# Written order on ACT, DVE and SP beside PE, and another order of the seven products, in a decoder block on one Trainium2 core

## The chip, the core and the metric

The kernel runs on one core of a Trainium2 chip. The core has five engines with a queue each: PE (TensorE, matmuls), ACT (ScalarE), DVE (VectorE), POOL (GpSimd) and SP (SyncE), and 16 DMA engines that move data between HBM and the on-chip memory. The metric is the device time of one execution, in microseconds. Timed twice, the kernel before took 1585.59 us in the median (1584.92 and 1586.26).

## What is computed

One decoder layer on 256 positions of 2048 channels, in float32:

```python
h = rmsnorm(x, norm_g)
proj = h @ w_in                          # 2048 x 18432, cut into 14 pieces
ya = stick_breaking(a_q, a_k, a_v)                       * silu(a_g)   # 8 heads of 128
yb = silu(layernorm(causal_conv31(b_a * sigmoid(b_b))))  * silu(b_g)
yc = gelu(c_u) * (tril(sgu_w) @ layernorm(gelu(c_v)) + sgu_b) * silu(c_g)
yd = dilated_mixture(d_q, d_k, d_v)                      * silu(d_g)   # 3 groups x 8 heads
gates = sigmoid(h @ w_gate + b_gate)     # 2048 x 8192, one gate per branch and channel
merged = sum(gates[n] * (y[n] @ w_branch[n]) for n in "abcd")
return rmsnorm(x + merged @ w_out, final_g)
```

In the stick-breaking attention `w[t, s]` is beta(t, s) times the product of 1 - beta(t, j) over s < j < t; it needs softplus and a running sum over keys. The dilated mixture is a softmax over three strided sets of keys.

## The kernel before

**Weights.** All weights are cut into 256 tiles of 128 x 2048 float32 (1 MB). A tile is loaded into one of six `st` buffers by a DMA that SP issues (`load_weights`, L85), and split into two float32r parts (`split`, L96): ACT copies it to `hi` (L97), DVE writes `lo = st - hi` (L98), with three buffers for each. A product then takes hi*hi + lo*hi + hi*lo.

**Kinds of work on PE.** `mm_t` (L212) multiplies one tile with all of `h` to give 128 channels of a projection, transposed: 16 pairs of a 512-column matmul (L219) and a 256-column one (L222). `proj_t` (L234) does two such tiles, adds the two halves of the result on DVE (L243) after a copy on ACT (L242), applies the activation functions, and calls `step`. `mm_n` (L251) is used where positions are the rows: four blocks of weights times two blocks of positions times three parts, 24 matmuls (L259 to L261), for the first projection `d_v`, the branches and the output.

**The seven products.** The gates (`gate_group`) and the projections `a_v` and `c_v` (`v_group`) go through `group` (L324). It forms a 2 x 2 block product with seven block products instead of eight, in Winograd's way: the sums s1, s2, s3, n4 of blocks of `h` are made once (`make_sx`, L293), the sums of weight tiles by DVE (`add_to`, L340; L342) in place, in the two tiles `ts` that a group holds to its end. Each product takes two halves of 12 matmuls (`half`, L331; L337), so a group has 14 halves; there are ten groups. The accumulators are X, Z and Y, in PSUM; `keep` (L344) copies one to an `so` buffer (five of them) by ACT and `done` (L350) adds or subtracts the rest on DVE (L353). `group` is a generator; `step(n)` runs n halves from the front of `queue`, so halves are mixed among other work: six per `proj_t` in head 7 and in the `b_g` gates, three per `proj_t` in the a heads, one per tile in the branches, one or two per `proj_t` in the `c_u` and `c_g` projections. What is left in the queue is run without other work between.

**Order of the whole.** The `d_v` projection and the norm (`make_h`, L183); the projections for the convolution, whose 248 taps DVE works off in between; the eight dilated heads (`d_head`, L556), the convolution's norm (`conv_norm`, L619) and `make_sx` among them; the `b_g` gates; branch d; the a heads in pairs (`a_pair`, L676); branches b and a; the norm of `c_v` (L731 to L754) and `c_mix`; branch c, whose sums are transposed by `turn` (L782); the output projection, `finish` and `store`. A branch (`branch`, L464) reads its y back from DRAM in one piece (`yf`), splits it into `yh` and `yl` (in the two `ph` buffers), and adds gate times product to a running sum in DRAM; the gates come back as `gl`, the sum as `ml`, by DMAs that POOL issues.

**What sets the order.** PE runs in the order in which the program is written. For ACT, DVE, SP and POOL a planner in the compiler chooses the order, by its own model of the times and by priorities that the program gives: `SPLIT_AHEAD` 100 for splits and evictions, `ADD_AHEAD` 140 for the sums of tiles, `CHAIN_AHEAD` 600 for the small stages that `later` and `tick` put off by some projections, `CONV_BEHIND` 100 below the rest for the taps. The result is a fixed list for each engine; an engine runs its list in order.

Of the kernel before, what the change touches and what calls it, by code (L numbers as in the profile page):

```python
# [9 lines left out]
F32 = mybir.dt.float32  # L10
# [16 lines left out]
SPLIT_AHEAD = 100  # L27
CHAIN_AHEAD = 600
ADD_AHEAD = 140
CONV_BEHIND = 100  # L30
# [27 lines left out]
def hybrid_block(ctx: ExitStack, tc, w, x, xT, vec, bg, cst, dmask, sgu_wT, sgu_lg, sgu_lb, sgu_b, final_g, out):  # L58
# [21 lines left out]
    ctx.enter_context(tc.manual_schedule(engines={mybir.EngineType.PE}))  # L80
# [3 lines left out]

    def load_weights(expect, pieces=1, between=None, again=False):  # L85
        assert again == (expect in used), expect
        used.add(expect)
        st = st_p.tile([P, 2048], F32, tag="st", name="st")
        n = 2048 // pieces
        for c in range(pieces):  # L90
            nc.sync.dma_start(st[:, c * n:(c + 1) * n], w[index[expect]][:, c * n:(c + 1) * n])
            if between is not None:
                between(c)
        return st
# [5 lines left out]
    def new_hi():  # L100
        return hi_p.tile([P, 2048], F32R, tag="hi", name="hi")[:]

    def new_lo():
        return lo_p.tile([P, 2048], F32R, tag="lo", name="lo")[:]

    def split_tile(st):
        hi, lo = new_hi(), new_lo()
        with tc.high_priority(SPLIT_AHEAD):
            split(hi, lo, st[:])
        return hi, lo  # L110

    def next_weights(expect):
        return split_tile(load_weights(expect))

    pending = []

    def later(n, fn):

        pending.append([n, fn])

    def tick():
        due = []
        for e in list(pending):
            e[0] -= 1
            if e[0] <= 0:
                pending.remove(e)
                due.append(e[1])
        for fn in due:
            with tc.high_priority(CHAIN_AHEAD):
                fn()  # L130

# [51 lines left out]
    def make_h():  # L183

        nc.sync.dma_start(cst_sb[:], cst[:, 0:C_K])
        red, rd2 = (so_p.tile([P, 2, S], F32, tag="so", name=n) for n in ("red", "rd2"))
# [6 lines left out]
        yield  # L193
# [4 lines left out]
        for q in range(4):  # L198
            for k in range(4 * q, 4 * q + 4):
                xk = xt[k // 8][:, k % 8, :]  # L200
                V.scalar_tensor_tensor(xk, xk, norm_g(k), rstd[:], op0=ALU.mult, op1=ALU.mult)
            ks = slice(4 * q, 4 * q + 4)
            split(xhl[:, ks, 0:S], xhl[:, ks, S:2 * S], xt[q // 2][:, 4 * (q % 2):4 * (q % 2) + 4, :])
        yield
# [4 lines left out]
        yield  # L209
# [24 lines left out]
    def proj_t(e0, e1, funcs=(None, None), n=0):  # L234

        dst = qk_p.tile([P, 2, S], F32, tag="qk", name="dst")
        for j, e in enumerate((e0, e1)):
            ps = ps_t.tile([P, 512], F32, tag="t", name="ps")
            mm_t(ps, next_weights(e), xhl)
            with tc.high_priority(SPLIT_AHEAD):  # L240
                bt = ev_p.tile([P, S], F32, tag="bt", name="bt")
                A.activation(bt[:], ps[:, S:2 * S], AF.Copy)  # L242
                V.tensor_add(dst[:, j, :], ps[:, 0:S], bt[:])  # L243
                if funcs[j] is not None:
                    A.activation(dst[:, j, :], dst[:, j, :], funcs[j])
            step((n + 1) // 2 if j == 0 else n // 2)
        tick()
        return dst
# [22 lines left out]
    def first_weights(q, expect):  # L271

        if q == 0:
            st = load_weights(expect, 4, lambda c: load_x(2 * c, 2) if c < 2 else None)
        elif q == 1:
            st = load_weights(expect, 2, lambda c: load_x(4 + 4 * c, 4))
        else:
            st = load_weights(expect, 1, lambda c: load_x(12, 4) if q == 2 else None)
        n = 512 if q == 0 else 1024
        hi, lo = new_hi(), new_lo()  # L280
        for o in range(0, 2048, n):
            for k in range(n // 512):
                split_x(4 * q + o // 512 + k)
            split(hi[:, o:o + n], lo[:, o:o + n], st[:, o:o + n])
        return hi, lo
# [7 lines left out]
    def make_sx():  # L293

        def quarter(k0, t0, name):
            q = st_p.tile([P, KB, P], F32, tag="st", name=name)
            V.tensor_add(q[:], xhl[:, k0:k0 + KB, t0:t0 + P].bitcast(F32), xhl[:, k0:k0 + KB, S + t0:S + t0 + P].bitcast(F32))
            return q
# [6 lines left out]
        a21 = quarter(0, P, "a21")  # L305
        a11 = quarter(0, 0, "a11")
        a22 = quarter(KB, P, "a22")
        V.tensor_sub(a22[:], a21[:], a22[:])
        put("s1", a22[:])
        V.tensor_sub(a22[:], a22[:], a11[:])  # L310
        put("s2", a22[:])
        V.tensor_sub(a11[:], a11[:], a21[:])
        put("s3", a11[:])
        a12 = quarter(KB, 0, "a12")
        V.tensor_add(a12[:], a12[:], a22[:])
        put("n4", a12[:])
# [7 lines left out]
    def group(expect, sink, bias=None):  # L324


        def tile_of(c, h, j):
            e = expect(c, 2 * h + j)
            return load_weights(e, again=e in used)

        def half(ps, st, name, j, first, last):  # L331
            lh = x_part(name)
            hi, lo = split_tile(st)
            for kk in range(4):
                k, o = 4 * j + kk, kk * 512
                for i, (part, w_) in enumerate(((0, hi), (0, lo), (1, hi))):
                    T.matmul(ps[:], lh(k, part), w_[:, o:o + 512], start=first and j == kk == i == 0,  # L337
                             stop=last and j == 1 and kk == 3 and i == 2, skip_group_check=name not in ("a11", "s1", "a12"))

        def add_to(st, other):  # L340
            with tc.high_priority(ADD_AHEAD):
                V.tensor_add(st[:], st[:], other[:])  # L342

        def keep(ps, name):  # L344
            t = so_p.tile([P, 512], F32, tag="so", name=name)
            with tc.high_priority(SPLIT_AHEAD):
                A.activation(t[:], ps[:], AF.Copy)
            return t

        def done(tb, c, op, a, b, t):  # L350
            with tc.high_priority(SPLIT_AHEAD):
                if op is not None:
                    op(t[:], a[:], b[:])  # L353
                sink(tb, c, t, op is not None)

        X = ps_x.tile([P, 512], F32, tag="x", name="X")
        if bias is not None:
            T.matmul(X[:], sel[:, bias:bias + 1].to_broadcast([P, P]), bgr[:], start=True, stop=False)
        ts = []
        for j in range(2):  # L360
            ts.append(tile_of(0, 0, j))
            half(X, ts[j], "a11", j, bias is None, True)
            yield
        p1 = keep(X, "p1")
        Z = ps_n.tile([P, 512], F32, tag="n", name="Z")
        if bias is not None:
            T.matmul(Z[:], sel[:, bias + 8:bias + 9].to_broadcast([P, P]), bgr[:], start=True, stop=False)
        for j in range(2):
            add_to(ts[j], tile_of(1, 0, j))
            half(Z, ts[j], "s1", j, bias is None, True)  # L370
            yield
        p5 = keep(Z, "p5")
        for j in range(2):
            add_to(ts[j], tile_of(1, 1, j))
            half(X, ts[j], "s2", j, False, True)
            yield
        u2 = keep(X, "u2")
        for j in range(2):
            t3, b22 = tile_of(1, 0, j), tile_of(1, 1, j)
            half(Z, b22, "n4", j, False, True)  # L380
            add_to(t3, b22)
            yield
            half(X, t3, "s3", j, False, True)
            if j == 0:
                yield
        done(0, 1, V.tensor_sub, Z, u2, u2)
        done(1, 1, V.tensor_sub, p5, X, p5)
        yield
        Y = ps_n.tile([P, 512], F32, tag="n", name="Y")
        for j in range(2):  # L390
            b21 = tile_of(0, 1, j)
            half(Y, b21, "a12", j, True, True)
            add_to(ts[j], b21)
            yield
            half(X, ts[j], "a22", j, False, True)
            if j == 0:
                yield
        done(0, 0, V.tensor_add, Y, p1, p1)
        done(1, 0, None, X, X, X)
        yield  # L400

    queue = []

    def step(n=1):

# [518 lines left out]
```

## Time and profile before

| | |
|---|---|
| median of two runs | 1585.59 us |
| the profiled execution, and its span | 1585.26 us, 1583.4 us |
| PE busy | 1465.1 us (93%) |
| DVE busy | 1241.8 us (78%) |
| ACT busy | 864.5 us (55%) |
| POOL busy | 87.5 us (6%) |
| granted TensorE clock, mean | 0.969 |
| moved by DMA | 370.89 MB, 234 GB/s over the span |

The span runs from the first to the last instruction of the program. Busy times come from the profiled execution. Matmuls are pipelined and overlap, so a busy PE need not be PE at its peak. In a row of instructions the name left of `<-` is the tile written, those right of it are read; `x320` is a count, then come busy microseconds, the mean nanoseconds of one, and the engine's idle time just before them with what ended it.

### The profile page before, as it was taken

To read this page: it belongs to the slowest core of one execution; us is meant where nothing else is said; L and a number is where in the kernel's file an instruction comes from. 1 tells how busy PE (TensorE), PEld (TensorE's weight loads), DVE (VectorE), ACT (ScalarE), POOL (GpSimd) and SP (SyncE) were. 2 spreads that over 40 slices of the span, in tenths; PEclk is the share of its full clock that TensorE was granted. 3 is DMA by queue.
4 is the path that set the end of the run, shared out by engine and by line. 5 is a ranking of instruction groups with operands and counts; after the bars stand their busy time and mean duration, and the time that the engine had idled before them with its cause. 6 is when DMAs were issued, how large, how long until landed. Compare 5 with 4: busy or idle time off the path is not lost.

```text
span 1583.4 us, 18121 instructions
## 1 busy us (share of the span) xinstructions
PE 1465.1 (93%) x7204; PEld 1225.5 (77%) x7204; DVE 1241.8 (78%) x1232; ACT 864.5 (55%) x777; POOL 87.5 (6%) x159
## 2 busy tenths in 40 slices
PE   7999999999999999869999999989989899959897
PEld 6788887888887777658788788867768688847786
DVE  7799999555799998867788788898889777866454
ACT  6544444353457567644466766766554477744251
POOL 0100000000000000010100000000211200011000
PEclk9999999999999999989999999989999999979999
DMA  9655543555166768677876757677898877578441
GB/s 358 217 211 186 186 176 136 180 180 181 59 237 257 283 249 289 212 276 275 283 282 224 241 213 279 239 260 256 301 337 297 328 274 248 196 282 299 167 161 54
DMA packets 62836, 370.89 MB, mean 234 GB/s; under 512 B 8128, under 2 KB 8256, under 8 KB 24096
## 3 DMA queue, kind: packets, MB, share of 16 engines
q1 hardware_dynamic: 44640, 313.68, 54.9%
q0 software_dynamic: 12784, 46.61, 8.8%
q10 hardware_dynamic: 5328, 9.45, 1.7%
q8 instruction: 56, 0.92, 0.2%
q14 instruction: 28, 0.23, 0.0%
HBM read 343.50 MB, written 26.21 MB: 233 GB/s over the span
## 4 chain that ended last, share of the span: by engine, by line
PE 62%; DVE 14%; DMA 10%; issue 7%; ACT 6%; POOL 0%; DVEq 0%; ACTq 0%; POOLq 0%; SPq 0%
PE ps L219 24%; PE ps L222 12%; DVE lo L98 8%; PE X L337 7%; DMA st<-in_w_dram 6%; ACT hi L97 3%; DVE st L342 3%; PE Z L337 3%; PE Y L337 2%; PE pso L261 2%; PE pso L260 2%; PE pso L259 2%; PE psy L259 1%; PE psy L260 1%; PE psy L261 1%
## 5 line engine op out<-in xcount | busy, mean ns | idle before, releaser
L98 DVE TENSOR_TENSOR lo<-st,hi 128x2048 fp32r<-128x2048 f32 (+2 forms) x318 | 711.6, 2247 | 165.7 <-ACT hi L97 164.9
L97 ACT ACTIVATE hi<-st 128x2048 fp32r<-128x2048 f32 (+2 forms) x318 | 595.0, 1879 | 231.4 <-PE psy L261 83.1
L219 PE MATMUL ps<-xhl,hi 128*128 128x512 f32 x1920 | 691.8, 403 | 6.3 <-ACT vd L523 3.8
L222 PE MATMUL ps<-xhl,lo 128*128 128x256 f32 x1920 | 523.4, 283 | 11.3 <-DVE lo L98 11.3
L219 PEld LDWEIGHTS ps<-xhl,hi 128*128 128x128 f32 x1920 | 361.6, 190 | 86.8 <-ACT vd L523 4.2
L222 PEld LDWEIGHTS ps<-xhl,lo 128*128 128x128 f32 x1920 | 366.2, 191 | 24.3 <-DVE lo L98 14.8
L242 ACT ACTIVATE bt<-ps 128x256 f32<-128x256 f32 x120 | 46.0, 384 | 331.0 <-PE ps L219 329.4
L342 DVE TENSOR_TENSOR st<-st 128x2048 f32<-128x2048 f32 x80 | 182.9, 2287 | 33.9 <-DMA st<-in_w_dram 33.5
L337 PE MATMUL X<-hi,xhl 128*128 128x512 f32 x320 | 109.2, 406 | 12.8 <-ACT hi L97 10.9
L337 PE MATMUL X<-hi,s 128*128 128x512 f32 x320 | 106.0, 393 | 0.9 <-ACT hi L97 0.9
L259 PE MATMUL psy<-hi,yh 128*128 128x512 f32 x256 | 100.6, 393 | 5.2 <-DVE ml L792 4.7
L260 PE MATMUL psy<-lo,yh 128*128 128x512 f32 x256 | 100.7, 393 | 1.6 <-DVE lo L98 1.6
L261 PE MATMUL psy<-hi,yl 128*128 128x512 f32 x256 | 100.2, 392 | 0.0
L243 DVE TENSOR_TENSOR dst<-ps,bt 128x256 f32<-128x256 f32 x120 | 50.5, 420 | 61.9 <-ACT bt L242 61.5
L543 DVE SCALAR_TENSOR_TENSOR cv<-glu,vec_sb,cv 128x246 f32<-128x246 f32 (+27 forms) x240 | 98.8, 462 | 0.2
L337 PEld LDWEIGHTS X<-hi,xhl 128*128 128x128 f32 x320 | 63.2, 197 | 27.2 <-ACT hi L97 11.6
L337 PE MATMUL X<-lo,xhl 128*128 128x512 f32 x160 | 65.1, 407 | 7.0 <-DVE lo L98 7.0
L337 PEld LDWEIGHTS X<-hi,s 128*128 128x128 f32 x320 | 60.7, 190 | 13.5 <-ACT hi L97 1.3
L337 PE MATMUL X<-lo,s 128*128 128x512 f32 x160 | 63.5, 397 | 5.6 <-DVE lo L98 5.6
L337 PE MATMUL Y<-hi,xhl 128*128 128x512 f32 x160 | 59.0, 432 | 3.4 <-ACT hi L97 3.4
L337 PE MATMUL Z<-hi,s 128*128 128x512 f32 x160 | 53.7, 400 | 8.7 <-ACT hi L97 8.7
L259 PEld LDWEIGHTS psy<-hi,yh 128*128 128x128 f32 x256 | 48.4, 189 | 16.3 <-DVE ml L792 4.9
(248 smaller groups left out, 1531.6 us busy)
## 6 DMA issues: line engine op xcount, KB each, us to landing
st<-in_w_dram SPq DMA_DIRECT2D x294, 1024.0 KB, 5.4
gl<-g_dr POOLq DMA_DIRECT2D x32, 256.0 KB, 6.8
m_dr<-gl POOLq DMA_DIRECT2D x24, 256.0 KB, 6.1
ml<-m_dr POOLq DMA_DIRECT2D x24, 256.0 KB, 6.3
g_dr<-p ACTq DMA_DIRECT2D x16, 256.0 KB, 4.5
g_dr<-u ACTq DMA_DIRECT2D x8, 256.0 KB, 5.2
g_dr<-g ACTq DMA_DIRECT2D x8, 256.0 KB, 3.9
xr<-in_x_dram POOLq DMA_DIRECT2D x8, 256.0 KB, 4.4
```

What stands on the lines that cost most here:

```text
L97: A.activation(hi, src, AF.Copy)
L98: V.tensor_sub(lo, src, hi.bitcast(F32))
L219: T.matmul(ps[:], hi[:, o:o + P], rhs[:, k, :], start=start, stop=stop)
L222: T.matmul(ps[:, 0:S], lo[:, o:o + P], rhs[:, k, 0:S], start=False, stop=False)
L242: A.activation(bt[:], ps[:, S:2 * S], AF.Copy)
L243: V.tensor_add(dst[:, j, :], ps[:, 0:S], bt[:])
L259: T.matmul(ps[tb][:], lh(k0 + kk, 0, tb), hi[:, o:o + 512], start=st, stop=False)
L260: T.matmul(ps[tb][:], lh(k0 + kk, 0, tb), lo[:, o:o + 512], start=False, stop=False)
L261: T.matmul(ps[tb][:], lh(k0 + kk, 1, tb), hi[:, o:o + 512], start=False, stop=sp)
L337: T.matmul(ps[:], lh(k, part), w_[:, o:o + 512], start=first and j == kk == i == 0, stop=last and j == 1 and kk == 3 and i == 2, skip_grou ...
L342: V.tensor_add(st[:], st[:], other[:])
L543: V.scalar_tensor_tensor(dst, src, wc, dst, op0=ALU.mult, op1=ALU.add)
```

## The change

- `manual_schedule` names PE, ACT, DVE and SP instead of PE alone, so all four run in the order in which the program issues. The priorities go. POOL's order is still chosen by the planner.
- All work becomes a list of `Job`s (`prog`): a load, a sum, a split, the matmuls, and what follows them. `run` goes through the list: at job t it issues the loads up to job t+5, the splits up to t+2, the sums up to t+4, then t's matmuls, its `post`, and what `later` put off to t.
- The seven products come in another order, X(a11), Y(a12), Z(s1), X(s2), then n4, s3, s3, n4, and X(a22) last. A group loads 14 tiles instead of 12, since the tiles of block (0,1) are loaded a second time for a22.
- Chains of small operations are cut into stages of about one engine each, one job apart: the stick-breaking softplus, the dilated softmax, the convolution's norm, `make_sx`, the norm of `c_v`; activation functions and gate sinks come one job after their eviction.
- The counts of halves between other work change: two before branch d and none extra inside a branch's start (before, three there, and up to 20 in branch c); one per `proj_t` in six of the eight `c` units instead of four. What is left runs in a row: ten halves before branch b, 16 before branch c.
- A branch's `yf` is fetched four jobs ahead of its place and split two ahead; `turn` comes two jobs after its sums; the norm of `h` is spread over the jobs of `d_v`.

```diff
-    ctx.enter_context(tc.manual_schedule(engines={mybir.EngineType.PE}))
+    ctx.enter_context(tc.manual_schedule(engines={mybir.EngineType.PE, mybir.EngineType.Activation, mybir.EngineType.DVE, mybir.EngineType.SP}))
...
+    class Job:
+        def do_load(self):
+            self.st = self.get(self.src) if self.src is not None else None
+            self.other = self.get(self.plus) if self.plus is not None else None
...
+        def do_add(self):
+            if self.other is not None:
+                V.tensor_add(self.st[:], self.st[:], self.other[:])
...
+    def later(n, fn):
+        calls.setdefault(now[0] + n, []).append(fn)
...
+    def run():
+        n = len(prog)
+        begun = [0, 0, 0]
+        while now[0] < n:
+            t = now[0]
+            for k, (ahead, name) in enumerate(((LOAD_AHEAD, "do_load"), (SPLIT_AHEAD, "do_split"), (ADD_AHEAD, "do_add"))):
+                while begun[k] < min(n, t + ahead + 1):
+                    getattr(prog[begun[k]], name)()
+                    begun[k] += 1
+            job = prog[t]
+            job.mm(*job.hl)
+            if job.post is not None:
+                job.post()
+            for fn in calls.pop(t, ()):
+                fn()
+            now[0] += 1
...
+        jobs = [half("X", "a11", j, tile_of(0, 0, j), first=True, keep=hold(ts, j),
+                     post=(lambda: keep(("X", "p1"))) if j else None) for j in range(2)]
+        jobs += [half("Y", "a12", j, tile_of(0, 1, j), first=True,
+                      post=(lambda: done(0, 0, V_.tensor_add, "Y", "p1", "p1")) if j else None) for j in range(2)]
+        jobs += [half("Z", "s1", j, lambda j=j: ts[j], plus=tile_of(1, 0, j), first=True,
+                      post=(lambda: keep(("Z", "p5"))) if j else None) for j in range(2)]
+        jobs += [half("X", "s2", j, lambda j=j: ts[j], plus=tile_of(1, 1, j),
+                      post=(lambda: keep(("X", "u2"))) if j else None) for j in range(2)]
...
+        jobs += [p3[0], p7[0], p7[1], p3[1]]
+        jobs += [half("X", "a22", j, lambda j=j: ts[j], plus=tile_of(0, 1, j),
+                      post=(lambda: done(1, 0, None, "X", "X", "X")) if j else None) for j in range(2)]
...
+        def fetch_y():
+            yf = box["yf"] = st_p.tile([P, 2048], F32, tag="st", name="yf")
+            nc.gpsimd.dma_start(yf[:], y_dr[b][:].rearrange("p k t -> p (k t)"))
...
+        job.do_add, job.split = fetch_y, cut
...
+    def v_out():
+        for c in range(2):
+            for tb in range(2):
+                t = so_p.tile([P, 512], F32, tag="so", name="vd")
+                A.activation(t[:], psv[c][tb][:], AF.Copy, scale=rstd_n[:, tb:tb + 1])
+                nc.gpsimd.dma_start(v_dr["d_v"][:, tb, c * 512:(c + 1) * 512], t[:])
+        gate_bias()
...
+    prog[3].post = h_squares
...
+    prog[4].post = lambda: (h_rms(), h_split(0))
+    prog[5].post = lambda: (h_split(1), h_split(2))
+    prog[6].post = lambda: (h_split(3), h_rstd())
+    prog[7].post = lambda: later(1, v_out)
...
                 A.activation(sp, sp, AF.Exp, scale=-1.0)
                 A.activation(sp, sp, AF.Ln, bias=1.0)
-                V.scalar_tensor_tensor(sp, zm, 0.0, sp, op0=ALU.max, op1=ALU.add)
-                split(sph, spl, sp)
-                later(1, sums)
+                later(1, softplus)
+
+        def softplus():
+            sp = box["sp"]
+            V.scalar_tensor_tensor(sp, box["zm"], 0.0, sp, op0=ALU.max, op1=ALU.add)
+            A.activation(box["sph"], sp, AF.Copy)
+            later(1, rest)
...
-        if tb and c:
-            turn(c - 1)
+        if tb:
+            later(2, lambda: turn(c))
```

More of the change, by code (lines that the diff above doesn't have):

```diff
@@ L100, in new_hi @@
     def new_hi():
-        return hi_p.tile([P, 2048], F32R, tag="hi", name="hi")[:]
+        return hi_p.tile([P, 2048], F32R, tag="hi", name="hi")
     def new_lo():
[L104 to L115, printed above, removed]
-    def later(n, fn):
-        pending.append([n, fn])
@@ L121, in tick, with load @@
[L121 to L129, printed above, removed]
-                fn()
+        return lo_p.tile([P, 2048], F32R, tag="lo", name="lo")
+    def load(expect):
+        used.add(expect)
+        st = st_p.tile([P, 2048], F32, tag="st", name="st")
+        nc.sync.dma_start(st[:], w[index[expect]])
+        return st
@@ new lines, in hybrid_block, with step @@
+    prog, queue, calls = [], [], {}
+    now = [0]
+    def later(n, fn):
+        calls.setdefault(now[0] + n, []).append(fn)
+    def step(n=1):
+        for _ in range(min(n, len(queue))):
+            prog.append(queue.pop(0))
+    def run():
[12 more added lines that the diff above has]
+            for fn in calls.pop(t, ()):
+                fn()
+            now[0] += 1
+        while calls:
+            for fn in calls.pop(now[0], ()):
+                fn()
+            now[0] += 1
@@ L232, in ft, with proj_t, mm, fn @@
         return ("in", OFF[name] // P + i)
[L234 to L240, printed above, removed]
+    def proj_t(e0, e1, hook, funcs=(None, None), n=0):
+        box = {}
+        def mm(j):
+            def fn(hi, lo):
+                if j == 0:
+                    box["dst"] = qk_p.tile([P, 2, S], F32, tag="qk", name="dst")
+                box["ps"] = ps_t.tile([P, 512], F32, tag="t", name="ps")
+                mm_t(box["ps"], (hi, lo), xhl)
+            return fn
+        def post(j):
+            def fn():
+                dst, ps = box["dst"], box["ps"]
                 bt = ev_p.tile([P, S], F32, tag="bt", name="bt")
@@ L324, in group @@
     def group(expect, sink, bias=None):
+        box, ts, bs = {}, {}, {}
         def tile_of(c, h, j):
[L328 to L338, printed above, removed]
@@ L356, in group @@
[L356 to L367, printed above, removed]
@@ L386, in group @@
[L386 to L399, printed above, removed]
@@ L400, in group, with keep @@
-        yield
-    queue = []
-    def step(n=1):
-        while n > 0 and queue:
-            try:
-                next(queue[0])
-                n -= 1
-            except StopIteration:
-                queue.pop(0)
+            return expect(c, 2 * h + j)
+        def keep(name):
+            t = box[name[1]] = so_p.tile([P, 512], F32, tag="so", name=name[1])
+            A.activation(t[:], box[name[0]][:], AF.Copy)
+        def done(tb, c, op, a, b, t):
+            if op is not None:
+                op(box[t][:], box[a][:], box[b][:])
+            sink(tb, c, box[t], op is not None)
@@ new lines, in half, with mm @@
+        def half(acc, name, j, src, plus=None, first=False, post=None, keep=None):
+            def mm(hi, lo):
+                lh = x_part(name)
+                if first and j == 0:
+                    pool, tag = (ps_x, "x") if acc == "X" else (ps_n, "n")
+                    ps = box[acc] = pool.tile([P, 512], F32, tag=tag, name=acc)
+                    if bias is not None and acc != "Y":
+                        r = bias + (8 if acc == "Z" else 0)
+                        T.matmul(ps[:], sel[:, r:r + 1].to_broadcast([P, P]), bgr[:], start=True, stop=False)
+                ps = box[acc]
+                fresh = first and j == 0 and (bias is None or acc == "Y")
+                for kk in range(4):
+                    k, o = 4 * j + kk, kk * 512
+                    for i, (part, w_) in enumerate(((0, hi), (0, lo), (1, hi))):
+                        T.matmul(ps[:], lh(k, part), w_[:, o:o + 512], start=fresh and kk == i == 0,
+                                 stop=j == 1 and kk == 3 and i == 2, skip_group_check=not first)
+            return Job(src, mm, plus=plus, post=post, keep=keep)
@@ L511, in hybrid_block @@
-    psv = [n_banks(c, "psv") for c in range(2)]
+                    if sink is None:
+                        nc.gpsimd.dma_start(m_dr[tb, :, o:o + 512], g[:])
+                    else:
+                        sink(c, tb, g)
+                if c < 3:
+                    fetch(c + 1)
+            return fn
+        prog.append(job_y(b, yhl))
+        for c in range(4):
+            for q in range(2):
+                prog.append(Job(("brN", bi, c, q), mm(c, q), post=post(c) if q else None))
+                step(n)
@@ new lines, in hybrid_block, with b_gate, hook, fn @@
+        d_head(h0 + 1, pair, 6 if h0 == 6 else 0)
+    def b_gate(i):
+        def hook(bg):
+            cn = qk_p.tile([P, 2, S], F32, tag="qk", name="cn")
+            nc.gpsimd.dma_start(cn[:], y_dr["b"][:, i:i + 2, :])
+            def fn():
+                V.tensor_mul(bg[:], bg[:], cn[:])
+                put_y("b", i, 2, bg[:])
+            later(3, fn)
+        proj_t(ft("b_g", i), ft("b_g", i + 1), hook, (AF.Silu, AF.Silu), n=6)
+    for i in range(0, 8, 2):
+        b_gate(i)
+    step(len(queue))
@@ L782, in turn @@
+    for i in range(8):
+        c_unit(i, 1 if i < 6 else 2)
+    step(len(queue))
+    mh, ml, held = [], [], {}
     def turn(c):
+        if c == 0:
+            mh.extend(s_p.tile([P, KB, S], F32R, tag="s", name=f"mh{i}") for i in range(2))
+            ml.extend(s_p.tile([P, KB, S], F32R, tag="s", name=f"ml{i}") for i in range(2))
         for f0 in (0, 2):
```

619 lines of the change are left out of this document (341 added, 278 removed).

## The prediction

> **What bounds the kernel now.** I read the page's busy shares first, then the timeline for the pace of PE without stalls, then the windows for the stretches where that pace is lost, last the waits.
>
> ```profile
> span 1583.4 us, 18121 instructions
> PE 1465.1 (93%) x7204; PEld 1225.5 (77%) x7204; DVE 1241.8 (78%) x1232; ACT 864.5 (55%) x777; POOL 87.5 (6%) x159
> ```
>
> PE leaves 118.3 us of the span idle (1583.4 - 1465.1). Its busy time overstates its work, since matmuls overlap; the true pace is in the starts of successive jobs. I call the 32 matmuls of `mm_t` on one weight tile a **T job**, the 12 of one half of a product a **half** (140 of them), and the 24 of `mm_n` an **N job**.
>
> ```profile
> 857.83 0.39 PE L219 MATMUL ps<-xhl,hi 128*128 128x512 f32 x1
> ...
> 863.48 0.40 PE L337 MATMUL Z<-hi,n 128*128 128x512 f32 x1
> ...
> 866.21 0.59 PE L682 MATMUL z<-dst 128*128 128x256 f32 x2
> ```
>
> A T job takes 863.48 - 857.83 = 5.65 us, a half 2.73, an N job of 24 twice that, 5.46. With this I price each stretch.
>
> ```profile
> 188.00:426.60 238.60, 232.77 (x1322) 203.08 (x1321) 172.47 (x314) 103.45 (x114) 2.57 (x4) 0.99 0.44 159
> 426.60:466.30 39.70, 37.48 (x214) 32.25 (x212) 35.83 (x42) 23.78 (x27) 0.05 (x1) 1.00 0.49 173
> 466.30:688.70 222.40, 205.29 (x987) 169.38 (x986) 198.58 (x152) 142.96 (x127) 7.76 (x14) 0.98 0.74 265
> 688.70:716.00 27.30, 13.58 (x43) 9.81 (x42) 18.28 (x10) 11.91 (x9) 3.96 (x7) 0.75 0.65 245
> 716.00:779.00 63.00, 62.74 (x277) 51.36 (x275) 46.04 (x26) 31.43 (x19) 7.06 (x13) 1.00 0.79 282
> 779.00:787.00 8.00, 4.99 (x16) 3.69 (x15) 8.00 (x7) 2.85 (x4) 1.48 (x3) 0.79 0.65 232
> 787.00:1041.00 254.00, 248.99 (x1282) 211.59 (x1281) 209.34 (x134) 175.01 (x149) 2.92 (x6) 0.99 0.69 245
> 1041.00:1091.00 50.00, 41.10 (x166) 32.45 (x165) 41.69 (x28) 34.06 (x28) 3.80 (x7) 0.86 0.70 241
> ...
> 1157.00:1178.00 21.00, 15.26 (x53) 11.74 (x52) 18.03 (x12) 10.10 (x7) 3.00 (x6) 0.84 0.90 332
> 1178.00:1244.00 66.00, 65.75 (x290) 54.07 (x289) 57.88 (x48) 31.87 (x21) 13.65 (x26) 1.00 0.90 322
> 1244.00:1275.00 31.00, 24.19 (x111) 19.45 (x110) 21.63 (x17) 15.33 (x15) 5.52 (x7) 0.89 0.86 308
> ...
> 1381.00:1426.00 45.00, 28.25 (x108) 22.10 (x107) 30.64 (x24) 20.56 (x16) 6.11 (x11) 0.81 0.76 270
> 1426.00:1499.00 73.00, 66.48 (x298) 53.82 (x296) 40.67 (x35) 27.79 (x22) 6.44 (x12) 0.98 0.69 234
> 1499.00:1583.40 84.40, 73.48 (x312) 60.03 (x310) 40.37 (x47) 27.49 (x32) 2.16 (x4) 0.93 0.33 113
> ```
>
> Columns: window; length; busy PE, PEld, DVE, ACT, POOL; granted clock; DMA share; GB/s. From 716 to 779 eight N jobs and seven halves need 62.8 us and take 63.0: interleaved so, PE runs at its pace. The losses sit where halves come thick or where something joins: head 7 and the `b_g` gates (466 to 689), branch d's start (689 to 716), the end of the a heads (1041 to 1091), branch b to a (1157 to 1178), the layer norm of `c_v` (1244 to 1275), the halves before branch c (1381 to 1426), the transposes (1426 to 1499). In most of these rows the granted clock falls to 0.75 to 0.89 with the idle time.
>
> ```profile
> L98 DVE TENSOR_TENSOR lo<-st,hi 128x2048 fp32r<-128x2048 f32 x308 | 701.8, 2288 | 159.4 <-ACT hi L97 158.6
> ...
> L97 ACT ACTIVATE hi<-st 128x2048 fp32r<-128x2048 f32 x308 | 586.5, 1911 | 228.7 <-PE psy L261 83.1 <-PE pso L261 24.5 <-DVE st L342 20.1
> ...
> L342 DVE TENSOR_TENSOR st<-st 128x2048 f32<-128x2048 f32 x80 | 182.9, 2287 | 33.9 <-DMA st<-in_w_dram 33.5
> ...
> L243 DVE TENSOR_TENSOR dst<-ps,bt 128x256 f32<-128x256 f32 x120 | 50.5, 420 | 61.9 <-ACT bt L242 61.5
> ...
> L353 DVE TENSOR_TENSOR u<-Z,u 128x512 f32<-128x512 f32 x10 | 6.8, 683 | 0.0
> ```
>
> These rows say why. A half costs DVE one split (2.29), 8/14 of a sum (1.31) and 3/14 of a closing sum (0.15): 3.74 us against 2.73 on PE. A T job costs it 2.29 + 0.42 = 2.71 against 5.65. So halves in a run are bound by DVE, and mixed 1:1 with T or N jobs by PE.
>
> **The change, part by part.** All matmuls stay, and all sums: eight per group (two each for s1, s2, s3, a22), in ten groups. PE's work is unchanged; what moves is who waits for whom. In the written order, DVE's list of step t is lo(t+2), sum(t+4), the eviction of t, then the small stages; ACT's is hi(t+2), eviction, stages. With three hi/lo buffers hi(t+2) waits for matmuls t-1; from there 1.91 + 2.29 = 4.2 us lead to a finished split while PE has two jobs in hand, 5.46 us at least. So the scheme carries itself, as long as nothing in a list waits long. Terms, after minus before:
>
> *Start, +10.* The four squares' reductions are now written behind the fourth job and its splits:
>
> ```profile
> 15.46 2.02 DVE red L190
> ...
> 20.14 2.02 DVE rd L190
> ...
> 26.00 1.95 DVE rd L190
> ```
>
> Before, they filled DVE gaps up to 28 us. Now 4 x 2.02 + 0.7 stand in one piece behind a split, with the next split, the rsqrt chain (about 5 us) and the four h splits (about 4 each) behind them: some 6 us late for the first T job. Then `gate_bias` is written in step 8, right after the four `vd` copies:
>
> ```profile
> DVE b L428 <- DMA b<-in_bg_dram: 4.9, 1, 4.9
> v_dr_d_v<-vd POOLq DMA_DIRECT2D x4, 256.0 KB, 9.7
> ```
>
> Four vd and two b tiles need six of five so buffers, so b1 waits for a landing (9.7), and DVE with every split queued behind it waits along: some 10 us where 4.9 were, less the two jobs in hand. Between 0 and +20; I take +10.
>
> *Heads 0 to 6, -6.* The two rows to 466.3 have 8.0 us of PE idle. The split stages (softmax, transpose and values one step apart) take most; but the convolution's norm comes in head 6 in one piece, so from -8 to +10.
>
> *Head 7 and `b_g`, -13.* 14 T jobs and 42 halves need PE 79.1 + 114.7 + 4 of small ones, 198 us; DVE had 198.6 busy in 222.4 (89%). At 95% of DVE it takes 209. Bounds: 199 if DVE never rests, 239 at the 83% of the row 1041 to 1091, so -23 to +17.
>
> *Branch d's start, -20.* Three halves (8.2) took 27.3, one (2.7) took 8.0: 24.4 lost. The fetch of y is now written four jobs ahead, when head 7 is long done:
>
> ```profile
> yf<-y_dr_d POOLq DMA_DIRECT2D x1, 1024.0 KB, 6.7
> ```
>
> Four jobs are at least 10.9 us, so 6.7 are hidden; a DVE split of y (2.29) and the queue remain, 4. From -24 to -5.
>
> *a heads, +2.* 24 T jobs, 36 halves and 14 of small ones need 248 of 254. The softplus chain stands on ACT before a split; that may cost 1 to 4 us in each of four pairs: -6 to +16.
>
> *Before branch b, -2.* 12 halves (32.8, with 3.5 of small ones) took 50, so 14 are lost. Ten halves stand there now (56 less 2, 8 and 36): 10 x 1.01 plus some 2 of the last pair's stages, 12. -10 to +8.
>
> *b to a, -1.* ph has two buffers, so the new y's split waits for b's last matmuls whoever orders it; 21 us for four halves (10.9) showed it. -8 to +5.
>
> *Norm of c_v, -7.* 31 us for three T jobs and a half (19.7). It now stands two jobs behind its load and its parts one step apart. -11 to +4.
>
> *Before branch c, -6.* Eight halves (21.8) took 45. Now 16 stand there (42 less 8, 8 and 10): 16 x 1.01, less two jobs in hand, plus y's split: 17 lost instead of 23. -15 to +8. The Trainium skill ("Perfetto Trace Analysis", Optimization Strategy) says that regimes with different bounds are better interleaved; the trace agrees (716 to 779), it speaks against these 16, and by it alone the 8 further halves would cost 8.1 us, a sum of -43.
>
> *Transposes, -6; end, -2.* Eleven N jobs and four turns need 64.4 of 73; `turn` now comes two jobs after its sums. 0 to -9, and 0 to -4.
>
> *Loads, 0.* Each group loads 14 tiles instead of 12, 20 MB more on SP's queue.
>
> ```profile
> st<-in_w_dram SPq DMA_DIRECT2D x294, 1024.0 KB, 5.4
> ```
>
> At the 332 GB/s of 1157 to 1178 one costs 3.2 us, 63 in all if none is hidden. But from 1178 to 1244 DMA was 90% busy and PE idle for 0.25 us, so I take 0, nearest to that row. SP's list follows the jobs too: of six st buffers two hold `ts` through a group, so load t+5 goes out when lo(t+1) is done, about 8 us ahead of its sum, against 5.4 to land. Where it lands late, DVE's whole list waits; the 33.5 us behind DMA in the row of sums above are that price before, and I leave them as they are.
>
> **Sum:** 10 - 6 - 13 - 20 + 2 - 2 - 1 - 7 - 6 - 6 - 2 = -51. The profiled execution took 1585.3 us (1.9 outside its span; the median is 1585.6, so nothing turns on the choice): **1534 us**, 3.2% less. About 2% is what a measurement of this kernel can tell from no change, so the bounds are 1554 and 1617.
>
> **Rivals.** *DVE binds in any order:* only the join of branch d goes, the rest cancels: 1585 - 20 = 1565. For it: DVE's busy time is unchanged. Against: its idle time behind hi in the row above, 158.6 us, is a matter of order. *The change doesn't do all it says:* POOL's queue stays with the planner, and yf, gl, cn and v come through it; a fetch of y queued behind a late store brings the 20 us back: 1554. *The loads are not hidden:* 1534 + 63 = 1597. For it: 0.90 of DMA in the branches, where two more loads in 14 come; against: they are spread over stretches with 0.65 to 0.79. The Trainium skill ("DMA: Bandwidth & Descriptors", Where 436 GB/s comes from) puts HBM at about 358 GB/s for a core; the rows stay below, so by it the branches would have little left, and the case a little more weight. *Slower: ACT held for an so buffer.* A branch's column holds two gl being written out and two being fetched, a group up to two more: six for five. If ACT's `keep` must wait for the store, every hi behind it waits too.
>
> ```profile
> ACT u L347 <- DMA m_dr<-gl: 4.3, 1, 4.3
> m_dr<-gl POOLq DMA_DIRECT2D x24, 256.0 KB, 6.1
> ```
>
> It happened once before. At 12 columns x 6.1 it costs 73, and with 5 for each a pair 93: 1627. It decides where the wait outlasts the two jobs in hand, 5.46 us.
>
> **From these to the numbers.** Forecast (1495 to 1554) 0.50; better than 1495, with DVE never resting (-10), no late start (-10) and the joins at their good ends (-21), 0.06; DVE binds 0.12; POOL's queue 0.06; loads 0.12; ACT held 0.14. So faster 0.56, within 2% 0.30, slower 0.14. The range leaves out the slowest case and the best: 1495 to 1600; for the forecast alone 1495 to 1554.
>
> **What would show it.** After: no window with 11 us lost at branch d's start; DVE above 93% busy in head 7 and `b_g`; a first T job some 6 us later and DVE's wait at b longer; 314 loads; PE still idle in the ten and the 16 halves. I would be wrong if DVE or ACT waited long and often on DMA landings, since in a written order all else waits behind.

## The result, and the profile after

The changed kernel took 1643.0 us in the median (1642.13 and 1643.87), 1.036 times the kernel before (95% interval 1.0318 to 1.0407): slower, where 1534 us and faster were forecast. The page of the kernel after, span and busy shares, then its groups of splits and sums, and its loads:

```profile
span 1642.2 us, 18166 instructions
...
PE 1475.0 (90%) x7204; PEld 1227.0 (75%) x7204; DVE 1262.8 (77%) x1232; ACT 862.5 (53%) x773; POOL 86.9 (5%) x160
...
L88 DVE TENSOR_TENSOR lo<-st,hi 128x2048 fp32r<-128x2048 f32 (+2 forms) x318 | 712.7, 2248 | 222.3 <-ACT hi L87 221.7
...
L87 ACT ACTIVATE hi<-st 128x2048 fp32r<-128x2048 f32 (+2 forms) x318 | 594.6, 1877 | 187.2 <-DVE st L120 64.8
...
L120 DVE TENSOR_TENSOR st<-st 128x2048 f32<-128x2048 f32 x80 | 182.8, 2286 | 18.9 <-DMA st<-in_w_dram 18.6
...
st<-in_w_dram SPq DMA_DIRECT2D x314, 1024.0 KB, 5.6
```

The work is the same: 7204 instructions counted on PE and 1232 on DVE, and ACT busy for 862 us where it was 864. DVE is busy for 21 us more with the same count, 13 of them in the taps (112.2 where 98.8 were). PE stands idle for 167 us instead of 118, DVE waits 222 us for `hi` ahead of its splits instead of 165. (Both sums include ten smaller splits; the prediction's row is of the whole tiles alone.) It is not the loads: DVE's wait for them ahead of the sums has halved (33.5 to 18.6).

The time by stage, from the start of a stage's first matmul on PE to the next one's, in the traces of before, after, and five of the experiments below:

| stage | before | after | e3 | e10 | e13 | e11 | e14 |
|---|---|---|---|---|---|---|---|
| up to the first T job | 61.9 | 60.4 | 62.6 | 58.4 | 61.5 | 59.9 | 56.5 |
| 16 T jobs of the convolution | 92.0 | 103.0 | 90.4 | 105.0 | 96.8 | 95.0 | 99.5 |
| heads 0 to 6 | 312.4 | 307.4 | 326.2 | 300.3 | 320.0 | 305.6 | 301.6 |
| head 7 and `b_g` | 213.9 | 243.9 | 244.0 | 234.9 | 234.4 | 216.2 | 209.7 |
| branch d with its start | 106.5 | 86.7 | 80.2 | 87.1 | 83.8 | 90.7 | 86.5 |
| a heads | 249.9 | 286.2 | 254.4 | 258.4 | 265.2 | 262.8 | 249.5 |
| before branch b | 54.7 | 58.6 | 48.4 | 52.6 | 49.7 | 44.2 | 44.0 |
| branches b and a | 152.8 | 145.5 | 137.5 | 146.3 | 145.0 | 145.2 | 142.1 |
| c units with the norm | 134.0 | 132.8 | 138.6 | 131.9 | 127.6 | 123.7 | 120.7 |
| halves before branch c | 47.8 | 67.4 | 62.7 | 62.3 | 65.8 | 65.9 | 64.8 |
| branch c to the end | 157.7 | 150.3 | 152.6 | 150.1 | 149.4 | 149.9 | 150.6 |

The row before branch c holds eight halves more after than before; branch d, the stretch before b, branches b and a, and the c units hold one, two, three and two fewer. Two stages carry the loss, head 7 with the `b_g` gates (+30) and the a heads (+36). Their windows after, and the same two before:

```profile
470.84:714.74 243.90, 204.05 (x951) 166.66 (x952) 204.34 (x153) 137.96 (x115) 4.85 (x9) 0.93 0.65 245
801.35:1087.53 286.18, 257.86 (x1271) 216.42 (x1271) 206.02 (x135) 176.13 (x150) 4.94 (x8) 0.95 0.65 238
```
```profile
466.26:680.13 213.87, 196.76 (x949) 162.35 (x948) 194.60 (x148) 139.54 (x122) 6.71 (x12) 0.98 0.73 265
786.59:1036.48 249.89, 244.88 (x1260) 208.07 (x1259) 205.23 (x131) 171.28 (x146) 3.12 (x5) 0.99 0.71 249
```

(Columns as in the prediction's windows.) No engine is full: in the a heads DVE is busy for 206 of 286 us, ACT for 176, as much as before in 250. The timeline of the kernel after at the first pair of a heads, ACT and then DVE (start, length, engine, line; in brackets the idle time before it and what ended it):

```profile
863.48 1.92 ACT L87 ACTIVATE hi<-st 128x2048 fp32r<-128x2048 f32 x1 [0.42 <-ACT p L486]
...
868.33 0.85 ACT L830 ACTIVATE ph_a<-ph_a 128x768 f32<-128x768 f32 x1 [2.92 <-DVE ph_a L828]
869.19 1.28 ACT L831 ACT_TABLE_LOAD   x1
870.48 0.84 ACT L831 ACTIVATE ph_a<-ph_a 128x768 f32<-128x768 f32 x1
871.35 1.28 ACT L832 ACT_TABLE_LOAD   x1
872.64 0.85 ACT L832 ACTIVATE ph_a<-ph_a 128x768 f32<-128x768 f32 x1
873.39 1.90 ACT L87 ACTIVATE hi<-st 128x2048 fp32r<-128x2048 f32 x1
...
881.04 0.84 ACT L838 ACTIVATE pr_a<-ph_a 128x768 fp32r<-128x768 f32 x1 [5.49 <-DVE ph_a L837]
881.79 1.89 ACT L87 ACTIVATE hi<-st 128x2048 fp32r<-128x2048 f32 x1
```
```profile
865.55 2.28 DVE L88 TENSOR_TENSOR lo<-st,hi 128x2048 fp32r<-128x2048 f32 x1
...
867.75 0.55 DVE L828 SCALAR_TENSOR_TENSOR ph_a<-z,ph_a 128x384 f32<-128x384 f32 x1
...
875.32 2.29 DVE L88 TENSOR_TENSOR lo<-st,hi 128x2048 fp32r<-128x2048 f32 x1 [7.03 <-ACT hi L87]
877.53 2.28 DVE L120 TENSOR_TENSOR st<-st 128x2048 f32<-128x2048 f32 x1
879.73 0.42 DVE L287 TENSOR_TENSOR dst<-ps,bt 128x256 f32<-128x256 f32 x1
880.06 0.95 DVE L837 SCALAR_TENSOR_TENSOR ph_a<-ph_a 128x768 f32<-128x768 f32 x1
883.72 2.29 DVE L88 TENSOR_TENSOR lo<-st,hi 128x2048 fp32r<-128x2048 f32 x1 [2.71 <-ACT hi L87]
```

Read the two together. ACT is through with `hi` at 865.4, and its next entry is Abs, which needs the masked scores; on DVE these stand behind a split (865.55 to 867.8), so ACT idles 2.92. Then Abs, Exp, Ln and two table loads take 5 us, with the next `hi` behind them; so DVE, whose next entry is that split, idles 7.03. Then the roles change again: ACT's copy (L838) waits 5.49 for softplus (L837), which stands behind a split, a sum and an eviction on DVE; DVE waits 2.71 for the `hi` behind the copy. From 865 to 884 the two engines work almost in turns, and PE has only two jobs in hand. The Trainium skill ("Perfetto Trace Analysis", Tensor Engine Instruction (MATMUL, LD_WEIGHTS)) calls ACT and DVE strictly first in, first out; the 2.92 and 5.49 us that ACT idles with a `hi` further on in its list agree.

### The profile page after: what moved, and what is told of

Read it like the earlier page. It is cut to its first block, busy times and chain, and to the rows that moved or that the text cites. A ratio compares the mean times of both kernels' runs of the same rounds, so it can differ in the third digit from the quotient of the medians.

```text
span 1642.2 us, 18166 instructions
## 1 busy us (share of the span) xinstructions
PE 1475.0 (90%) x7204; PEld 1227.0 (75%) x7204; DVE 1262.8 (77%) x1232; ACT 862.5 (53%) x773; POOL 86.9 (5%) x160
## 5 line engine op out<-in xcount | busy, mean ns | idle before, releaser
L87 ACT ACTIVATE hi<-st 128x2048 fp32r<-128x2048 f32 (+2 forms) x318 | 594.6, 1877 | 187.2 <-DVE st L120 64.8
L254 PEld LDWEIGHTS ps<-xhl,hi 128*128 128x128 f32 x1920 | 365.4, 192 | 94.7 <-DVE dst L287 12.2
L257 PEld LDWEIGHTS ps<-xhl,lo 128*128 128x128 f32 x1920 | 369.4, 192 | 33.5 <-DVE lo L88 24.9
L120 DVE TENSOR_TENSOR st<-st 128x2048 f32<-128x2048 f32 x80 | 182.8, 2286 | 18.9 <-DMA st<-in_w_dram 18.6
L637 DVE SCALAR_TENSOR_TENSOR cv<-glu,vec_sb,cv 128x255 f32<-128x255 f32 (+14 forms) x240 | 112.2, 468 | 6.6
L429 PEld LDWEIGHTS X<-hi,s 128*128 128x128 f32 x320 | 62.3, 195 | 19.7 <-ACT hi L87 7.2
L308 PEld LDWEIGHTS psy<-lo,yh 128*128 128x128 f32 x256 | 49.1, 192 | 19.4 <-DVE lo L88 9.6
L429 PE MATMUL Y<-hi,xhl 128*128 128x512 f32 x160 | 54.5, 406 | 5.7 <-ACT hi L87 5.7
```

The source lines that it names most:

```text
L87: A.activation(hi, src, AF.Copy)
L120: V.tensor_add(self.st[:], self.st[:], self.other[:])
L254: T.matmul(ps[:], hi[:, o:o + P], rhs[:, k, :], start=start, stop=stop)
L257: T.matmul(ps[:, 0:S], lo[:, o:o + P], rhs[:, k, 0:S], start=False, stop=False)
L308: T.matmul(ps[tb][:], lh(k0 + kk, 0, tb), lo[:, o:o + 512], start=False, stop=False)
L429: T.matmul(ps[:], lh(k, part), w_[:, o:o + 512], start=fresh and kk == i == 0, stop=j == 1 and kk == 3 and i == 2, skip_group_check=not first)
```

## The experiments

Five theories were at hand in the end. Theory 1: the lists of ACT and DVE wait for each other, as just read. Theory 2: the 20 more loads and the products' order. Theory 3: DVE binds anyhow. Theory 4 came after e4: PE's own list, in which the ends of the chains (`cc`, the sums over keys of the a heads, and `pp`, the transposes of the dilated heads) come too soon. Theory 5 came after e8: a written list loses whatever one step puts ahead of the next `hi` or `lo` beyond the slack, 5.46 - 4.2, some 1.3 us.

All runs but e12 and e14 were timed once. The kernel before took 1578 to 1591 us beside them, so 10 us between two single times tell little. The stages repeat better: in after, e2, e4 and e9, whose edits leave them alone, heads 0 to 6 took 307.4 us each time and the 16 T jobs 101.7 to 103.4.

**e1: splits one job further ahead**

```diff
-SPLIT_AHEAD = 2
+SPLIT_AHEAD = 3
```

> Splits are written three jobs ahead instead of two, so hi(t+3) and lo(t+3) stand ahead of the small stages of step t in both lists; nothing else changes. Theory 1 (in a step with a stage of two engines, DVE then ACT, the next hi stands behind the ACT stage and the next lo behind that hi, so the two lists wait for each other in turn): the stages now fall behind a split that is a job further on, and a good part of the 58 us comes back: 1590 to 1620 us. Theory 2 (the 20 more loads and the other order of the seven products cost it) and theory 3 (DVE binds in any order): no change, 1635 to 1650. It could also go the other way: with three buffers hi(t+3) waits for the matmuls of job t, and evictions stand behind it.

1836.2 us (before 1580.6). ACT's longest waits in this run (us in total, times, longest):

```profile
ACT hi L87 <- DVE st L120: 272.9, 63, 8.0
ACT hi L87 <- PE ps L254: 258.2, 70, 7.6
```

The other way was the one taken, far stronger than I thought: `hi` of t+3 waits for the matmuls of job t, and the eviction of t, written behind it, comes one split late. This tells nothing of the theories.

**e2: the stick-breaking stages cut further.** The dilated Exp, which the expectation names, was left where it was.

```diff
             if j:
-                A.activation(sp, zm, AF.Abs) ...
-                later(1, softplus)
+                later(1, trio)      # Abs, Exp, Ln; then later(1, softplus)
...
-            A.activation(box["sph"], sp, AF.Copy)     # now first in rest()
...
-            A.activation(zm, zm, AF.Exp)
-            later(1, values)
+            later(1, expo)          # Exp; then later(1, values)
```

> Only the stages of the two attentions are cut further: Abs, Exp and Ln come one step after the DVE operation that they read, softplus on DVE a step later, the copy to sph a step later with the subtraction behind it, the last Exp a step after its subtractions; the dilated softmax's Exp likewise. All the work stays. Theory 1: the a heads go from 291 us back towards the 254 of before, 255 to 268, and the whole to 1608 to 1620; head 7 and the b_g gates gain little, since their loss begins in the norm of the convolution. Theory 2 and 3: the a heads stay within 5 us of 291.

1633.1 us; the a heads 275.4: 11 us of the 36 came back, less than theory 1 gave.

**e3: ACT and DVE planned**

```diff
-engines={PE, Activation, DVE, SP}
+engines={PE, SP}
```

> The same program, with ACT and DVE given back to the planner (PE and SP stay in written order, no priorities). The products' order, the 314 loads, the stages and the counts of halves stay. Theory 1: ACT and DVE are no longer bound to the steps, so the a heads and head 7 with the b_g gates come back within 10 us of before, 1570 to 1610. Theory 2: the loss stays, 1630 or more. Theory 3: 1630 or more too.

1599.2 us, 44 less than after with the same program: the a heads come back to 254.4, the first T jobs to 90.4. The written order of ACT and DVE is the cause there, and theories 2 and 3, by which the loss would have stayed, do not carry it. Against theory 1, head 7 with `b_g` stays at 244.0, and heads 0 to 6, whose stages have no priority now, lose 14 us against before.

**e4: products and loads as before** (12 loads a group; n4, s3 by turns, then a12, a22 by turns)

> The order of the seven products of before, with 12 loads in a group instead of 14 (294 in all), everything else as in the kernel after. Theory 1: within 10 us of 1643. Theory 2: 1600 or less, most of it in head 7 and the b_g gates and in the a heads, where 78 of the 140 halves are. Theory 3: within 10 us of 1643.

1636.2 us, 7 less, which single times cannot tell from nothing; head 7 with `b_g` 242.9, the a heads 284.5, within 2 us of after. Theory 2 does not carry the 58 us.

**e5: `cc` and `pp` three jobs later**

```diff
-            later(1, transpose)
+            later(4, transpose)
...
-            later(1, sums)
+            later(4, sums)
```

> The kernel after with two numbers changed: in the a heads the sums (matmuls cc) come four jobs after the stage before them instead of one, and in the dilated heads the transposes (pp) four jobs after the softmax instead of one. No operation moves from one engine to another, and the DVE and ACT stages stay where they were. Theory 4 (PE's own list: cc and pp are written a fixed number of jobs behind their scores; where a job is a half of 2.73 us, PE reaches them before the chain on DVE and ACT is done and stands): the a heads go from 286 to 255 to 268, head 7 with the b_g gates from 244 to 220 to 230, the whole to 1595 to 1612. Theory 1 (DVE and ACT waiting for each other in the steps with a stage of both): these stages are where they were, so the a heads stay above 278 and the whole above 1630.

1635.3 us. The a heads take 285.8, as if nothing had been done:

```profile
793.78:1079.60 285.82, 258.75 (x1272) 215.28 (x1271) 206.23 (x135) 173.14 (x149) 4.94 (x8) 0.96 0.65 238
```

PE's waits at `cc` were where the lateness showed, not where it came from: now the half and the T job ahead of `cc` wait for their splits. Theory 4 falls there; head 7 with `b_g` gains 7 us (236.7).

**e6: the same with ACT and DVE planned,** and the start changed: each quarter's squares after its own job, `gate_bias` as `later(4, gate_bias)`.

> As the last, with ACT and DVE given back to the planner, and two changes at the start: the squares of x and their reductions one quarter after each of the first four jobs instead of all after the fourth, and the bias of the gates four jobs later. Theory 4: PE's waits for pp (38 us where ACT and DVE were planned without it) and for cc (13 us) go, 1599 less 40 to 45, and the start changes little under the planner: 1550 to 1565. Theory 1: ACT and DVE were already free of the steps, so within 10 us of 1599.

1566.8 us, just above the range of theory 4. Once ACT and DVE are free, the distance of `pp` does count: head 7 with `b_g` 220.7 instead of 244.0, heads 0 to 6 307.6 instead of 326.2. In the a heads a later `cc` gained nothing here either: they took 260.4 where e3 took 254.4, and PE waited 13.9 us one step further on, at the values, for ACT's last Exp.

**e7 and e8: everything at once in written order; e8 with e4's products.** All chains are cut so that ACT's part comes in the step after the DVE part it reads (`rsqrt` in two, `make_sx`'s splits a step later), with `pp` and `cc` later and e6's start. In both, the split that gives s1 came after its source was overwritten for s2, so the products with s1 use the values of s2; the operations and their number are the same.

> All four engines in written order, with everything at once: the later cc and pp, the stages cut so that no step has a DVE operation that an ACT operation of the same step waits for (attention, norm of the convolution, its block sums, norm of c_v), and the two changes at the start. Theory 4 with the start: about 20 us from head 7 and b_g, 30 from the a heads, 10 from the first sixteen T jobs: 1570 to 1590. Theory 1: most comes from the cutting of the stages, so clearly below the run with the later cc and pp alone, by more than 25 us.

> As the last, with the products' order and the 12 loads per group of before. Theory 2 (loads and products' order, which gave 7 us in the kernel after): 5 to 10 us below the last, in the branches and before branch b. If the loads cost nothing once PE no longer waits for its own list: within 3 us of the last.

1598.0 and 1577.2 us. The first is above theory 4's range and 37 below e5, as theory 1 had it (more than 25). Cutting took the a heads to 273.3 (e7) and 266.9 (e8), and 8 of the start's 10 us came back (95.3 in the first T jobs). The products' order with its loads, worth 7 us at most in e4, is worth 21 here, not in the branches as expected but mostly in head 7 with `b_g` (9) and the a heads (6). So theory 2 holds a part that the other waits had covered; whether loads or order, no run parts. In e8 s1 was late:

```profile
PE Z L448 <- ACT s L87: 16.6, 1, 16.6
```

**e9: e2 with Abs, Exp and Ln in three steps**

```diff
-                A.activation(sp, sp, AF.Exp, scale=-1.0)
-                A.activation(sp, sp, AF.Ln, bias=1.0)
-                later(1, softplus)
+                later(1, lambda: A.activation(sp, sp, AF.Exp, scale=-1.0))
+                later(2, lambda: A.activation(sp, sp, AF.Ln, bias=1.0))
+                later(3, softplus)
```

> As the kernel in which only the stages of the stick-breaking attention were cut, with Abs, Exp and Ln on ACT in three steps instead of one. There the loss that is left in the a heads, 5 to 6 us a pair, stands in the half and the T job behind the last scores, where Abs, Exp, Ln and two table loads (5 us) stand in one piece ahead of the next hi. Theory 5 (a written list loses whatever one step puts ahead of the next hi or lo beyond the slack of two jobs in hand, 5.46 us less 4.2 for hi and lo, about 1.3): the a heads go from 275 to 255 to 260, the whole to 1612 to 1620. Theory 1 in its narrow form (only a DVE stage with an ACT stage behind it in one step costs time): the a heads stay above 270.

1617.2 us; the a heads 269.6, 6 less than e2 where 15 to 20 were expected. That lies between theory 5 (255 to 260) and theory 1 in its narrow form (above 270): the piece of 5 us costs something, but the pieces are not all.

**e10 and e13: the kernel after with ACT alone, then DVE alone, given back to the planner**

> The kernel after with ACT alone given back to the planner; PE, DVE and SP stay in written order. Theory 5: ACT's pieces are the long ones in the a heads (Abs, Exp, Ln, Exp), so freeing ACT alone lets hi go first and brings the a heads to 258 to 266 and the whole to 1600 to 1620. If it is DVE's list that holds the splits, the a heads stay above 275.

> The mirror of the run in which ACT alone went back to the planner: the kernel after with DVE alone given back; PE, ACT and SP stay in written order. If ACT's written list is where the time goes (ACT freed gave 54 us): the a heads stay above 275 and the whole above 1625. If either list alone is enough to untie the two: the a heads at 255 to 265, the whole at 1585 to 1605.

1589.2 and 1600.8 us: 54 and 42 less than after, by one word each. The first is below the 1600 to 1620 expected; the second is what was expected if either list alone is enough. The a heads in the one and the other:

```profile
785.71:1044.13 258.42, 248.57 (x1271) 209.43 (x1270) 204.91 (x134) 173.18 (x147) 3.87 (x6) 0.99 0.72 263
```
```profile
796.53:1061.70 265.17, 250.75 (x1271) 210.48 (x1270) 206.08 (x134) 175.40 (x150) 4.87 (x8) 0.99 0.69 260
```

The same place as above in e10's ACT:

```profile
843.69 1.92 ACT L87 ACTIVATE hi<-st 128x2048 fp32r<-128x2048 f32 x1
846.54 1.92 ACT L87 ACTIVATE hi<-st 128x2048 fp32r<-128x2048 f32 x1 [0.93 <-DVE st L120]
849.48 0.85 ACT L830 ACTIVATE ph_a<-ph_a 128x768 f32<-128x768 f32 x1 [1.03 <-DVE ph_a L828]
```

The planner puts one more `hi` ahead of Abs. ACT waits 1.03 us for the scores instead of 2.92, and DVE has that `hi` while ACT works off its 5 us. So either list alone, freed, unties most of it; it takes both in written order to lose 36 us.

**e11 and e12: small pieces, all in written order.** e8 with e9's three steps, `cc` six jobs behind the scores, and `make_sx` from head 5 on, about one operation or split a step; e12 with seven halves moved from before branch c into the c units.

> All four engines in written order, with the stages cut to pieces of at most about 2.5 us on one engine in a step: Abs, Exp and Ln in three steps, the other stages cut as in the run with everything at once, cc six jobs behind the scores and pp four behind the softmax, the block sums s1 to n4 one operation or one split a step from head 5 on, the products' order and 12 loads of before, the two changes at the start. Theory 5: written order as such costs nothing, so the a heads come to 248 to 256, head 7 and b_g to 205 to 215, the whole to 1535 to 1555. If written order as such costs (theory 1 in its wide form): the whole stays above 1565.

> As the last, and the halves before branch c are spread: three for each of the first three c units, then two for three and one for two, so nine stand before branch c instead of 16 (two products of c_mix a little later). Seven halves at 4.1 us each in a run become seven at 2.7 among T jobs, and the fill of the c units' stalls: 10 to 18 us less than the last, 1520 to 1540. If the c units are bound by DVE or DMA already: within 5 us of the last.

e11 took 1560.8 us: head 7 with `b_g` 216.2, the a heads 262.8 (205 to 215 and 248 to 256 were expected), so theory 5 came near and a part of the loss stayed. e12 took 1570.1, 0.9895 of before (0.9851 to 0.9939), 9 us above e11's single time. By stages the c units hold eight halves more and take 28.3 us more, 3.5 each; the run before branch c is 23.6 shorter, not the 30 that eight halves at 3.74 would give; and branch c to the end takes 5.0 more. Spreading them brought nothing. One reason is in the trace: the shorter run no longer covers the fetch of y, for which ACT waits 12.4 us in e12 and not at all in e11, and PE waits 9.4 at branch c's first matmul for the `hi` behind it. In the c units PE waits 9.3 us for `lo` where e11 waits 2.0; why DVE comes late there is open.

**e14 and e15: e11 with ACT planned, then ACT and DVE**

> The kernel whose stages are cut to small pieces (1561 us with all four engines in written order), with ACT given back to the planner. If what is left of the loss there (the a heads at 263 where 250 were, the three first branches at 69 to 74 where 64 to 66 were) is again ACT's order: a heads 250 to 257, branches 64 to 68, the whole 1535 to 1550. If pieces of that size already cost nothing on ACT: within 6 us of 1561.

> The same program with ACT and DVE both given back to the planner. If DVE's written order costs something of its own: 5 to 15 us below the run with ACT alone planned. If it costs nothing, or the planner's own misjudgements weigh as much: within 5 us of it, or above.

e14 took 1529.9 us, **0.966 of before (0.9625 to 0.970)**, the fastest of all and below what was expected. e15 took 1537.5, so beside a planned ACT, DVE's written order showed no cost. DVE is busy for as long in e14 (1261.0 us) as in the kernel after (1262.8), and for longer than before, so theory 3 falls for good. The page of e14, and its a heads:

```profile
span 1525.5 us, 18112 instructions
...
PE 1445.1 (95%) x7204; PEld 1211.5 (79%) x7204; DVE 1261.0 (83%) x1232; ACT 858.0 (56%) x770; POOL 88.3 (6%) x160
```
```profile
753.82:1003.35 249.53, 246.26 (x1272) 208.61 (x1271) 208.91 (x137) 166.85 (x143) 3.85 (x6) 1.00 0.70 253
```

Against e11 the 33 us lie in many stages, most in the a heads (13) and head 7 (6).

## Why the prediction was wrong

The step that failed is the sentence "the scheme carries itself, as long as nothing in a list waits long". It set 4.2 us for `hi` and `lo` against 5.46 us in hand and so left 1.3 us, and then priced each chain by itself. A step that puts an ACT operation behind a DVE operation of the same step, and a `hi` behind that, can spend far more than this (7.03 us on DVE, above), and the stages that the change calls one engine's are often of two.

- *a heads,* +2, at worst +16: measured +36. "1 to 4 us in each of four pairs" was mis-sized: it is 9 in the mean. The term prices the chain on ACT alone, without ACT's wait for the scores ahead of it and without the second turn at softplus. e10 and e13 show that this is order; e5, that it is not PE's.
- *Head 7 and `b_g`,* -13, up to +17: measured +30. The step "at 95% of DVE" failed: DVE was busy for 204 of 244 us. At its beginning `make_sx` and head 6's softmax go through both lists as in the a heads, and PE's own list reaches the transposes too soon:

```profile
504.40 0.45 PE L699 MATMUL pp<-cst_sb,ph_d 128*128 128x128 f32 x1 [13.47 <-ACT p L408]
```
```profile
489.54 1.06 ACT L87 ACTIVATE s<-a 128x1024 fp32r<-128x1024 f32 x1 [3.56 <-DVE a L381]
...
501.03 1.06 ACT L87 ACTIVATE n<-a 128x1024 fp32r<-128x1024 f32 x1 [4.75 <-DVE a L386]
```

  The softmax that `pp` reads runs on DVE at 503.3 to 505.4, behind those splits; the releaser that the row names is only the last semaphore. Neither is the whole cause: both lists freed left 244.0 (e3), a later `pp` alone 236.7 (e5), the two together gave 220.7 (e6). e11, in written order with the sums made earlier and `pp` later, takes 216.
- *Start,* +10: right in sum, +9.5, by luck. Some 6 us were forecast for a late first T job. It began 1.5 earlier, waited 1.8 for its `lo` and ran at a granted clock of 0.55 over its first 7 us (0.76 before), and the second began 1.4 late. DVE's wait for b was as forecast (10.6), but less of it was hidden: the third and fourth T jobs took 8.2 us more than 5.65 each. The two waits on a landing, here and at the norm of `c_v`:

```profile
DVE b L475 <- DMA b<-in_bg_dram: 10.6, 1, 10.6
DVE bst L907 <- DMA vc<-v_dr_c_v: 8.2, 1, 8.2
```

- *Branch d,* -20: -19.8, of which a half that stands elsewhere is 2.7. *Heads 0 to 6,* -6: -5. *Transposes and end,* -8: -7.4. Right.
- *Before branch c,* -6: 19.6 more for eight halves (21.8 at PE's pace), so -2. (The prediction's own parts, 16.2 less 5.5 plus 4.2 for y's split, give 15 lost, not 17.) *Before b,* -2: +3.9 with two halves fewer (5.5), so about +9, the same lists again (e3 48.4). *b to a,* -1: -7.3 with three halves fewer (8.2), so about +1.
- *Norm of `c_v`,* -7: -1.2 with two halves fewer, so about +4. Being early in the list did not help where the reload of `vc` landed late (8.2 us, above).
- *Loads,* 0: right in the kernel after, by DVE's wait. The rival (1597) had a mechanism that e8 may show, at a third of its price and together with the products' order. The 358 GB/s that the prediction names there were no ceiling: from 1477 to 1519 us the kernel after moved 396 GB/s.
- The rival on the slow side (ACT held for an `so` buffer, 1627) named another wait. It came near the time, not the cause: in the kernel after, ACT waits 2.3 us in all for stores of such buffers. (With small pieces and before's products, in e11, it waits 22.9.) The rival *DVE binds in any order* falls with e14, and POOL's queue did not bring branch d's 20 us back. What I said would make me wrong were long and frequent waits on DMA landings. There were two long ones (above); most of the rest were waits of the two lists on each other.

## What to carry to other kernels

When two engines pass work back and forth, a written order on both can make a place in one list a wait in the other: follow, on paper, what stands behind each waiting entry on both sides, over two or three steps, not each chain alone. Cut stages where the work changes engine, keep the pieces small (here 1.3 us of slack was left of 5.46; no run had pieces as short as that), and try leaving one of the lists to the planner, which cost one word and gave 54 us. Where PE waits is not where the time goes: in the a heads, moving `cc` moved the wait and nothing else.

## What was not expected of the hardware

Where PE stood more, the granted clock was lower: in the a heads 0.95 in the kernel after (PE busy for 258 of 286 us), 1.00 in e14 (246 of 250). A change of function set on ACT took 1.28 us with nothing behind it: Abs ends at 869.18, the load runs from 869.19, Exp starts at 870.48. The Trainium skill ("ScalarE: Activation LUTs", What ACT_TABLE_LOAD costs) counts some 1.38 us of drain beside it; the trace of this kernel does not show that.
